# Four more products with tokens stationary, and activations turned by VectorE and small DMAs on the way

## Chip, cores and metric

One NeuronCore of a Trainium2 chip runs the whole program in one launch. The metric is the device time of one execution in microseconds (us).

## What is computed

A transformer block with sliding-window attention is followed by a second block on the same 256 tokens of width 2048. The second one is what the change touches:

```python
g = sigmoid(gate_logits + b_gate)                # gate_logits: 4096 of the columns of h @ w_in
merged = g[..., 0, :] * (y_mla @ w_mla_proj) + g[..., 1, :] * (y_diff @ w_diff_proj)
x = x + merged @ w_out                           # 2048 x 2048
h2 = rmsnorm(x, ffn_norm_g)
x = x + (silu(h2 @ w_ffn_gate) * (h2 @ w_ffn_up)) @ w_ffn_down
return rmsnorm(x, final_norm_g)
```

All data is float32. A product is made of three passes on TensorE: both operands are split into a high part and a rest ("hi", "lo"), and hi·hi, lo·hi and hi·lo are added up in PSUM.

## The kernel before

**Weights.** 5440 tiles of 128x128 come from HBM in the order in which the program asks for them, as 340 chunks of 16 tiles (1 MB, queue of SP). `Weights.cut` makes of each chunk two halves of 8 tiles: ACT writes `w_hi` (L84), DVE writes `w_lo` (L85). There are four buffers of each, so the cast of a half waits until PE is done with the half four before it. Nothing on TensorE runs without both.

**Two forms of product.** `gemm` and `gemm4` (L319, L329) hold the weights stationary. The activations move, transposed (features on partitions) with hi and lo of all 256 tokens side by side: `w_hi` goes against 512 columns, `w_lo` against the 256 of hi, which is two matmuls for a tile of weights. Results come out with features on partitions. `gemm_nat` with `nat3` (L367, L378) holds the activations of 128 tokens stationary, and 512 columns of weights move: six matmuls of 512 columns for four tiles (three passes, two blocks of tokens). Results come out with tokens on partitions. They must be turned before they can be stationary operands of the next product.

**Turning.** `moved` (L434) issues 16 DMAs of 32x128 on POOL's queue; with a DVE transpose inside 32x32 blocks ahead of it, this turns a 128x512 tile.

**Order around the change.** 512 tiles of gate, 256 of `mla`, 256 of `diff` and 256 of `out` use the first form, the `ffn` (1408 tiles) and `down` (704) the second. Gate strips of 128 features are evacuated by `total`, `scaled` and `gate` (L390, L395, L874); the loop at L880 interleaves the MLA and differential attention with these products through `between`, to which generators are added that emit a piece of work every few tiles. After `diff` a result is gated, added to the MLA part and split into `mg` (L919 to L932). After `out` (L938 to L946), each strip is added to the residual, scaled with the norm's gains and split into `h3_*`, the moving operand of the ffn stage; no turn is needed, since `h` is already there with features on partitions, and its 128-token slices serve as stationary operands. `after_out` (L950) sums the squares on PE, takes the root on POOL, and turns the residual (`x_t` to `x2n`) during the ffn. There, `split_act` (L967) splits the turned products (`act_hi`, `act_lo`).

The framework's scheduler fixes each engine's own order of instructions ahead of the run; the engine follows it strictly.

Of the kernel before, what the change touches and what calls it, by code (L numbers as in the profile page):

```python
# [14 lines left out]
P = 128  # L15
# [152 lines left out]


@with_exitstack  # L170
def block_kernel(ctx, tc, order, w, x01, xt, bc, fg, cst, out):
# [10 lines left out]
    def unit(name, dt=F32):  # L182
        return up.tile([P, 512], dt, name=name, tag="u", bufs=NU)
# [7 lines left out]
    def half(t, i):  # L191
        return t[:, (i % 2) * S:(i % 2) * S + S]
# [185 lines left out]
    def gemm_nat(name, col, acts):  # L378
# [492 lines left out]
    hb = const.tile([P, 32], F32, name="hb")  # L871
    nc.vector.tensor_scalar(out=hb, in0=colt[:, B_GATE:B_GATE + 32], scalar1=0.5, scalar2=None, op0=ALU.mult)

    def gate(m, o):  # L874
        ps = gemm("gate", m, h)
        scaled(o, ps, rb_2)
        nc.scalar.activation(out=o, in_=o, func=AF.Tanh, scale=0.5, bias=hb[:, m:m + 1])

    mer = []
    for u in range(4):  # L880
        qk = []
        for c in (0, 16):
            for i in range(4):
                ps = gemm("dqk", c + 4 * u + i, h)
                if i % 2 == 0:
                    qk.append(unit("qk_d"))
                scaled(half(qk[-1], i), ps, rb_2)
        pp = gemm_nat("dv", u * 512, h)
        v = []
        for tb in range(2):  # L890
            vh, vl = unit("v_hi", F32R), unit("v_lo", F32R)
            nc.scalar.activation(out=vh, in_=pp[tb], func=AF.Copy, scale=r_2[:, tb:tb + 1])
            nc.vector.scalar_tensor_tensor(out=vl, in0=pp[tb], scalar=r_2[:, tb:tb + 1], in1=vh.bitcast(F32),
                                           op0=ALU.mult, op1=ALU.subtract)
            v.append((vh, vl))
        if u == 0:
            between.drain()
            between.every, between.apart = 8, 3
        for i in range(2):
            between.add(attend_d(2 * u + i, qk[i], qk[2 + i], [(half(a, i), half(b, i)) for a, b in v]))  # L900
        if u == 0:
            for m in range(16):
                if m % 2 == 0:
                    t2, m2 = unit("gate"), unit("m")
                gate(m, half(t2, m))
                ps = gemm("mla", m, y_m)
                t = half(m2, m)
                total(t, ps)
                nc.vector.scalar_tensor_tensor(out=t, in0=half(t2, m), scalar=1.0, in1=t, op0=ALU.add, op1=ALU.mult)
                mer.append(t)  # L910

    gates = []
    for m in range(16):
        if m % 2 == 0:
            t2 = unit("gate")
        gate(16 + m, half(t2, m))
        gates.append(half(t2, m))
    between.drain()
    mg = []  # L919
    for m in range(16):  # L920
        ps = gemm("diff", m, y_d)
        if m % 2 == 0:
            t2 = unit("md")
        t = half(t2, m)
        total(t, ps)
        nc.vector.scalar_tensor_tensor(out=t, in0=gates[m], scalar=1.0, in1=t, op0=ALU.add, op1=ALU.mult)
        tt(t, t, mer[m], ALU.add)
        hl = unit(f"mg{m}", F32R)
        nc.scalar.activation(out=hl[:, 0:S], in_=t, func=AF.Copy, scale=0.5)
# [18 lines left out]
    x2n = []  # L948

    def after_out():  # L950
        yield
        nc.vector.tensor_copy(out=r_3, in_=rstd(sq.sums(), D))
        for cb in range(4):
            for tb in range(2):
                yield 8 if x2n else 3
                tr = unit("x2_t")
                for i in range(4):
                    nc.vector.transpose(
                        out=tr.rearrange("p (a m j) -> p a m j", a=4, m=4)[:, :, i, :],
                        in_=x2[4 * cb + i][:, tb * P:tb * P + P].rearrange("p (a j) -> p a j", a=4))  # L960
                x2n.append(moved(tr, "x2n"))

    between.every, between.apart = 16, 1
    between.add(after_out())
    act = [None] * KF

    def split_act(u, parts):  # L967
        yield 5
        hls = []
        for t in parts:  # L970
            t = t.rearrange("p (a g i) -> p g a i", a=4, g=4)
            hi, lo = unit("act_hi", F32R), unit("act_lo", F32R)
            nc.scalar.copy(out=hi.rearrange("p (g a i) -> p g a i", a=4, g=4), in_=t)
            tt(lo.rearrange("p (g a i) -> p g a i", a=4, g=4), t,
               hi.bitcast(F32).rearrange("p (g a i) -> p g a i", a=4, g=4), ALU.subtract)
            hls.append((hi, lo))
        for k in range(4):
            q = slice(k * P, k * P + P)
            act[4 * u + k] = [(hi[:, q], lo[:, q]) for hi, lo in hls]

    for u in range(KF // 4):

        parts = []
        for tb, ps in enumerate(gemm_nat("ffn", u * 512, h)):
# [3 lines left out]
        for tb, ps in enumerate(gemm_nat("ffn", DFF + u * 512, h)):  # L988
            z = parts[tb]
            tt(z, ps, z, ALU.mult)  # L990
            tr = unit("ffn_t")
            nc.vector.transpose(out=tr, in_=z)
            parts[tb] = moved(tr, "ffn_m")
        between.add(split_act(u, parts))
# [96 lines left out]
def _matrices(i):  # L1091

    pairs = []
    for j in range(16):
        kt = j // 8
        for hd in (16 * kt + j % 8, 16 * kt + 8 + j % 8):
            pairs.extend(range(hd * 64, hd * 64 + 64))
    pairs = np.array(pairs)
    in_a, in_2 = i["w_in_a"][0], i["w_in_2"][0]
    uq = i["w_uq_2"][0].reshape(768, 16, 192)  # L1100
    ukv = i["w_ukv_2"][0].reshape(512, 16, 256)
    kpe = in_2[:, 1280:1344]
    ffn = np.concatenate([i["w_ffn_gate_2"][0], i["w_ffn_up_2"][0]], axis=1)[:, _quarters(2 * DFF)]
    return {
        "in_a": np.concatenate([in_a[:, :2048][:, pairs], in_a[:, 2048:2560], in_a[:, 2560:][:, pairs]], axis=1),
        "out_a": i["w_out_a"][0][pairs],
        "in_2": in_2[:, :1280],
        "kpe": np.concatenate([kpe, kpe], axis=1),
        "dqk": in_2[:, 1344:5440],
        "dv": in_2[:, 5440:7488],  # L1110
        "gate": in_2[:, 7488:],
        "uq": np.concatenate([uq[:, :, :128].reshape(768, -1), uq[:, :, 128:].reshape(768, -1)], axis=1),
        "uk": ukv[:, :, :128].reshape(512, -1),
        "uv": ukv[:, :, 128:].reshape(512, -1),
        "mla": i["w_mla_proj_2"][0],
        "diff": i["w_diff_proj_2"][0],
        "out": i["w_out_2"][0],
        "ffn": ffn,
        "down": i["w_ffn_down_2"][0][:, _quarters(D)],
    }  # L1120
# [36 lines left out]
```

## Time and profile before

| | us |
|---|---|
| median of three runs (2012.25 to 2013.1) | 2012.4 |
| the profiled execution | 2012.29 |
| its span, first to last instruction | 2010.4 |
| PE busy in it | 1991.8 |
| DVE, ACT, POOL busy | 1265.3, 1036.5, 253.4 |

The span is the sum over a chain of work that ends with the last instruction. A stage can be read by itself: with the borders of the stages (the first matmul on the next operand), the profile gives for each the length, how long every engine was busy, and the number of instructions. Where PE is busy for the whole stage, the stage's length is that of its matmuls; a wait that PE gets there is added to the end of the program.

### The profile page before, as it was taken

To read this page: it belongs to the slowest core of one execution; us is meant where nothing else is said; L and a number is where in the kernel's file an instruction comes from. 1 tells how busy PE (TensorE), PEld (TensorE's weight loads), DVE (VectorE), ACT (ScalarE), POOL (GpSimd) and SP (SyncE) were. 2 spreads that over 40 slices of the span, in tenths; PEclk is the share of its full clock that TensorE was granted. 3 is DMA by queue.
4 is the path that set the end of the run, shared out by engine and by line. 5 is a ranking of instruction groups with operands and counts; after the bars stand their busy time and mean duration, and the time that the engine had idled before them with its cause. 6 is when DMAs were issued, how large, how long until landed. Compare 5 with 4: busy or idle time off the path is not lost.

```text
span 2010.4 us, 27424 instructions
## 1 busy us (share of the span) xinstructions
PE 1991.8 (99%) x10600; PEld 1703.7 (85%) x10600; DVE 1265.3 (63%) x2026; ACT 1036.5 (52%) x1681; POOL 253.4 (13%) x505
## 2 busy tenths in 40 slices
PE   9999999999999999999999999999999999999997
PEld 8888888888888888888888888888888888888886
DVE  7778766887857555566575767655555555554543
ACT  6777655656546444455465445544444444434443
POOL 0000000000000000000000000154555543330000
PEclk9999999999999999999999999999999999999999
DMA  7444455444344555545545555565566555565552
GB/s 301 153 145 148 168 207 180 161 153 147 131 174 163 191 189 190 194 163 181 181 160 191 187 195 189 184 222 204 207 217 216 208 206 208 209 220 190 196 200 85
DMA packets 68596, 372.68 MB, mean 185 GB/s; under 512 B 13745, under 2 KB 21937, under 8 KB 25329
## 3 DMA queue, kind: packets, MB, share of 16 engines
q1 hardware_dynamic: 51552, 359.76, 50.0%
q0 software_dynamic: 15760, 9.21, 1.6%
q10 hardware_dynamic: 1152, 1.97, 0.3%
q8 instruction: 83, 1.36, 0.3%
q14 instruction: 49, 0.39, 0.1%
HBM read 360.91 MB, written 2.10 MB: 181 GB/s over the span
## 4 chain that ended last, share of the span: by engine, by line
PE 96%; DVE 2%; ACT 1%; issue 1%; DMA 0%; POOL 0%; POOLq 0%; SPq 0%; ACTq 0%
PE ps_g L198 89%; PE ps_s L198 4%; PE ps_t L198 2%; PE ps_t L426 1%; DVE rope_t L201 1%; DVE w_lo L85 0%; DVE k_n L201 0%; DVE q_r L201 0%; DMA w_raw<-w 0%; ACT w_hi L84 0%; PE ps_t L865 0%; ACT prob L417 0%; PE ps_t L841 0%; DVE prob L411 0%; DVE y_m L235 0%
## 5 line engine op out<-in xcount | busy, mean ns | idle before, releaser
L85 DVE TENSOR_TENSOR w_lo<-w_raw,w_hi 128x1024 fp32r<-128x1024 f32 (+1 forms) x677 | 824.0, 1219 | 471.3 <-ACT w_hi L84 457.5
L84 ACT CAST w_hi<-w_raw 128x1024 fp32r<-128x1024 f32 (+1 forms) x677 | 708.7, 1048 | 571.5 <-PE ps_g L198 513.5
L198 PE MATMUL ps_g<-w_hi,h 128*128 128x512 f32 x1664 | 513.5, 389 | 0.0
L198 PE MATMUL ps_g<-h,w_hi 128*128 128x512 f32 x1672 | 410.3, 393 | 0.6 <-DVE h L238 0.6
L198 PEld LDWEIGHTS ps_g<-w_hi,h 128*128 128x128 f32 x1664 | 312.3, 188 | 64.9
L198 PEld LDWEIGHTS ps_g<-h,w_hi 128*128 128x128 f32 x1672 | 306.2, 188 | 63.1 <-issue 3.5
L198 PE MATMUL ps_g<-w_lo,h 128*128 128x512 f32 x832 | 323.7, 389 | 0.0
L198 PE MATMUL ps_g<-h,w_lo 128*128 128x256 f32 x1672 | 223.1, 284 | 0.0
L198 PEld LDWEIGHTS ps_g<-h,w_lo 128*128 128x128 f32 x1672 | 214.3, 191 | 10.4 <-issue 3.2
L439 POOL DMA_DIRECT2D ffn_m<-ffn_t x352 | 172.3, 497 | 222.8 <-ACT w_hi L84 86.1
L198 PEld LDWEIGHTS ps_g<-w_lo,h 128*128 128x128 f32 x832 | 156.2, 188 | 32.4
L279 POOL TENSOR_TENSOR rstd<-ms,mhalf 128x2 f32<-128x2 f32 x14 | 14.2, 1012 | 1217.2 <-DVE ms L274 1199.6
L198 PE MATMUL ps_g<-w_hi,act_hi 128*128 128x512 f32 x344 | 133.8, 389 | 0.0
L198 PE MATMUL ps_g<-w_lo,act_hi 128*128 128x512 f32 x344 | 133.8, 389 | 0.0
L198 PE MATMUL ps_g<-w_hi,act_lo 128*128 128x512 f32 x344 | 133.8, 389 | 0.0
L198 PEld LDWEIGHTS ps_g<-w_lo,act_hi 128*128 128x128 f32 x344 | 64.6, 188 | 13.5
L198 PEld LDWEIGHTS ps_g<-w_hi,act_hi 128*128 128x128 f32 x344 | 64.6, 188 | 13.5
L198 PEld LDWEIGHTS ps_g<-w_hi,act_lo 128*128 128x128 f32 x344 | 64.6, 188 | 13.2
L439 POOL DMA_DIRECT2D x2n<-x_t x128 | 62.7, 497 | 31.7 <-ACT ffn L986 15.6
L198 PE MATMUL ps_g<-y_m,w_hi 128*128 128x512 f32 x256 | 63.8, 391 | 0.0
L198 PE MATMUL ps_g<-y_d,w_hi 128*128 128x512 f32 x256 | 61.2, 391 | 0.0
L198 PE MATMUL ps_g<-g,w_hi 128*128 128x512 f32 (+1 forms) x240 | 57.8, 377 | 0.0
(254 smaller groups left out, 2011.6 us busy)
## 6 DMA issues: line engine op xcount, KB each, us to landing
w_raw<-w SPq DMA_DIRECT2D x337, 1024.0 KB, 4.8
ffn_m<-ffn_t POOLq DMA_DIRECT2D x352, 16.0 KB, 4.1
w_raw<-w SPq DMA_DIRECT2D x5, 512.0 KB, 7.6
x2n<-x_t POOLq DMA_DIRECT2D x128, 16.0 KB, 4.1
x_t<-xt SPq DMA_DIRECT2D x7, 256.0 KB, 7.6
fgt<-fg POOLq DMA_DIRECT2D x4, 256.0 KB, 3.9
out<-x2n SPq DMA_DIRECT2D x4, 256.0 KB, 3.1
out<-x2n ACTq DMA_DIRECT2D x4, 256.0 KB, 3.5
```

What stands on the lines that cost most here:

```text
L84: a = nc.scalar.copy(out=hi[:, q], in_=src[:, q])
L85: b = nc.vector.tensor_tensor(out=lo[:, q], in0=src[:, q], in1=hi.bitcast(F32)[:, q], op=ALU.subtract)
L198: nc.tensor.matmul(out=o, lhsT=a, rhs=b, start=start, stop=stop, skip_group_check=True)
L201: nc.vector.tensor_tensor(out=o, in0=a, in1=b, op=op)
L279: nc.gpsimd.tensor_tensor(out=r, in0=t, in1=mhalf[:, 0:n], op=ALU.pow)
L426: nc.tensor.transpose(out=ps[:, j * P:j * P + P], in_=p[:, j * P:j * P + P], identity=ident)
L439: nc.gpsimd.dma_start(out=o[32 * b:32 * b + 32, a * P:a * P + P], in_=tr[32 * a:32 * a + 32, b * P:b * P + P])
```

## The change

- Gate, `mla`, `diff` and `out` use `gemm_nat`; weights of these four are reordered so that the features of a strip of 512 come out in the order that the later turn wants.
- The gate's bias is no column any more but a row, copied to all partitions. `row` fetches 128x512 (256 KB) on POOL's queue into a buffer; the norm's gains ahead of the ffn (`R_FFN`) come in the same way.
- `turn_residual` turns the residual `x1` to `x1n` during the gate and `mla` products (DVE transposes and 16 DMAs, eight times). Before, the same work on `x2` was in the ffn.
- A strip of `diff` is gated and added with tokens on partitions, then `turned` (one transpose and 16 DMAs for a block of tokens, 32 a strip) and split by `split_turned` into `t_hi` and `t_lo`, the stationary operands of `out`. A strip of `out` goes the same way (`residual_2`), with the gains multiplied in (`x2g`), to become those of the ffn. It takes four strips of turned activations to make all 16 pieces along k.
- The first product after such a turn (`out`, and the gate and up product of the ffn) begins with two strips side by side: `gemm_nats` runs pieces 0 to 11 along k of both, then pieces 12 to 15 of both. 
- The sums of squares are collected by ACT (`accum_out`), and four matmuls that added them up are gone.

```diff
+    def gemm_nats(name, cols, acts, late):
+        banks = [[bank("g") for _ in range(2)] for _ in cols]
+        n = len(acts)
...
+        for ks in (range(late), range(late, n)):
+            for col, pp in zip(cols, banks):
+                for k in ks:
+                    hi, lo = W.take(name, k * P, col, 4)
+                    for tb in range(2):
+                        nat3(pp[tb], acts[k], tb, hi, lo, k == 0, k == n - 1)
+                    between.tiles(4)
+        return banks
+    def turned(z):
+        tr = unit("turn")
+        nc.vector.transpose(out=tr, in_=z)
+        return moved(tr, "turned")
+    def split_turned(acts, k0, parts):
+        yield 5
...
+            nc.scalar.copy(out=oh, in_=t)
+            tt(ol, t, oh.bitcast(F32), ALU.subtract)
...
+    def row(base, i):
+        t = unit("row")
+        nc.gpsimd.dma_start(out=t, in_=rw[:, base + i * 512:base + i * 512 + 512])
+        return t
...
-    mg = []
-    for m in range(16):
-        ps = gemm("diff", m, y_d)
...
+    for i in range(4):
+        parts = []
+        for tb, ps in enumerate(gemm_nat("diff", i * 512, y_d)):
+            t = gates[i][tb]
+            gated(t, ps)
+            tt(t, t, mer[i][tb], ALU.add)
+            parts.append(turned(t))
+        between.add(split_turned(mg, 4 * i, parts))
...
-    for m, ps in blocks("out", 0, 16, mg):
-        t = x1[m]
-        tt(t, t, ps[:, 0:S], ALU.add)
-        tt(t, t, ps[:, S:], ALU.add)
-        x2.append(t)
-        hl = unit(f"h3_{m}", F32R)
-        split_scaled(t, gcol(G_FFN, m), hl)
-        h.append(hl)
-        sq.add(t)
+    def residual_2(cb, pp):
+        g = row(R_FFN, cb)
+        parts = []
+        for tb, ps in enumerate(pp):
+            t = x2n[2 * cb + tb]
+            nc.vector.scalar_tensor_tensor(out=t, in0=ps, scalar=0.5, in1=t, op0=ALU.mult, op1=ALU.add)
+            z = unit("x2g")
+            nc.scalar.activation(out=z, in_=t, func=AF.Square, accum_out=sums3[:, 4 * tb + cb:4 * tb + cb + 1])
+            z = unit("x2g")
+            tt(z, t, g, ALU.mult)
+            parts.append(turned(z))
+        between.add(split_turned(h, 4 * cb, parts))
+
+    for cb, pp in enumerate(gemm_nats("out", [0, 512], mg, 12)):
+        residual_2(cb, pp)
+    for cb in (2, 3):
+        residual_2(cb, gemm_nat("out", cb * 512, mg))
...
+        if u == 0:
+            pg, pu = gemm_nats("ffn", [0, DFF], h, 12)
```

What the order of the instructions says of the place where `out` ends and the ffn begins. First POOL, whose queue carries the small DMAs. Before, from the last attention norms on to the first DMAs of the ffn:

```order
L279 TENSOR_TENSOR rstd_10067<-ms_10065,mhalf_115 128x2
L279 TENSOR_TENSOR rstd_12374<-ms_12372,mhalf_115 128x2
L439 DMA x2n_12490<-x2_t_12485 32x128 x16
L439 DMA ffn_m_12612<-ffn_t_12610 32x128 x16
L439 DMA ffn_m_12632<-ffn_t_12630 32x128 x16
```

Of the change, from the first strip of `out` to the last:

```order
L482 DMA row_11342<-rw 128x512
L454 DMA turned_11351<-turn_11349 32x128 x16
L454 DMA turned_11375<-turn_11373 32x128 x16
L482 DMA row_11392<-rw 128x512
L454 DMA turned_11401<-turn_11399 32x128 x16
L454 DMA turned_11425<-turn_11423 32x128 x16
L482 DMA row_11580<-rw 128x512
L454 DMA turned_11589<-turn_11587 32x128 x16
L454 DMA turned_11613<-turn_11611 32x128 x16
L482 DMA row_11784<-rw 128x512
L454 DMA turned_11793<-turn_11791 32x128 x16
L454 DMA turned_11817<-turn_11815 32x128 x16
```

The four strips of `out` each have a fetch of gains and 32 moves here, and each fetch stands behind the moves of the strip before it. None of these was there before.

Then DVE, before, around the first half of weights of the ffn (`w_lo_12338`, with the last strips of `out` still to be evacuated):

```order
L85 TENSOR_TENSOR w_lo_12338<-w_raw_12335,w_hi_12337 128x1024
L201 TENSOR_TENSOR y_2858<-y_2858,ps_g_12247 128x256 x2
L85 TENSOR_TENSOR w_lo_12354<-w_raw_12335,w_hi_12353 128x1024
L238 SCALAR_TENSOR_TENSOR h3_15_12292<-y_2858,x01t_75,h3_15_12292 128x256
L201 TENSOR_TENSOR sq_11660<-sq_11660,sq_12295 128x256
```

DVE of the change, from the first half of weights of the ffn (half 416 of the program, counted from 0; the three `w_lo` after it are 417, 418 and 419); `row_11580` is the gains of the third strip of `out`, `ps_g_11630` and `ps_g_11631` are the fourth strip, and `t_lo_11701` is the first strip's rest, an operand of the first product of the ffn:

```order
L86 TENSOR_TENSOR w_lo_11850<-w_raw_11847,w_hi_11849 128x1024
L202 TENSOR_TENSOR x2g_11585<-x1n_7340,row_11580 128x512
L461 STREAM_TRANSPOSE turn_11587<-x2g_11585 128x512
L86 TENSOR_TENSOR w_lo_11866<-w_raw_11847,w_hi_11865 128x1024
L202 TENSOR_TENSOR x2g_11609<-x1n_7504,row_11580 128x512
L461 STREAM_TRANSPOSE turn_11611<-x2g_11609 128x512
L86 TENSOR_TENSOR w_lo_11884<-w_raw_11881,w_hi_11883 128x1024
L994 SCALAR_TENSOR_TENSOR x1n_7670<-ps_g_11630,x1n_7670 128x512
L994 SCALAR_TENSOR_TENSOR x1n_7844<-ps_g_11631,x1n_7844 128x512
L86 TENSOR_TENSOR w_lo_11900<-w_raw_11881,w_hi_11899 128x1024
L202 TENSOR_TENSOR t_lo_11701<-turned_11351,t_hi_11700 128x512
L202 TENSOR_TENSOR t_lo_11705<-turned_11375,t_hi_11704 128x512
```

Between weights and operands of the next stage now stand instructions of the third and fourth strip of `out`. The first matmuls of the ffn on PE are, of the change:

```order
L199 MATMUL ps_g_11843<-w_hi_11849,t_hi_11700 128x512
L199 MATMUL ps_g_11843<-w_lo_11850,t_hi_11700 128x512
L199 MATMUL ps_g_11843<-w_hi_11849,t_lo_11701 128x512
L199 MATMUL ps_g_11844<-w_hi_11849,t_hi_11704 128x512
L199 MATMUL ps_g_11844<-w_lo_11850,t_hi_11704 128x512
```

Its third matmul takes the rest of the first turned strip, where before all operands were slices of `h3_*`.

## Rows read from the trace of the kernel before

**Rows 1.** The page's head and its busy times of the engines: busy us (share of the span) and number of instructions.
```profile
span 2010.4 us, 27424 instructions
PE 1991.8 (99%) x10600; PEld 1703.7 (85%) x10600; DVE 1265.3 (63%) x2026; ACT 1036.5 (52%) x1681; POOL 253.4 (13%) x505
```
**Rows 2.** The chain that ended last, by engine.
```profile
PE 96%; DVE 2%; ACT 1%; issue 1%; DMA 0%; POOL 0%; POOLq 0%; SPq 0%; ACTq 0%
```
**Rows 3.** Stages: start and end, length, then busy us (instructions) of PE, PEld, DVE, ACT and POOL, the granted clock, the DMA share and GB/s. In order: attention with the gate and `mla` products, the 256 tiles of `diff`, the 256 of `out`, the 1408 of the ffn.
```profile
516.00:1100.42 584.42, 584.04 (x3307) 511.90 (x3307) 367.95 (x588) 305.56 (x517) 9.14 (x8) 1.00 0.50 178
1100.42:1189.49 89.07, 89.07 (x514) 78.72 (x512) 62.08 (x94) 43.19 (x64) 0.00 (x0) 1.00 0.53 189
1189.49:1278.56 89.07, 89.07 (x513) 78.67 (x512) 62.11 (x95) 44.99 (x64) 0.00 (x0) 1.00 0.53 191
1278.56:1757.86 479.30, 479.30 (x2118) 396.88 (x2117) 259.24 (x275) 211.79 (x221) 220.04 (x449) 1.00 0.60 209
```
**Rows 4.** PE in order of time, at the end of `diff` and at the border of `out` and ffn: start, length of the group (to the end of its last matmul), what, and how many.
```profile
1185.74 2.08 PE L198 MATMUL ps_g<-y_d,w_lo 128*128 128x256 f32 x16
1187.65 2.00 PE L198 MATMUL ps_g<-y_d,w_hi 128*128 128x512 f32 x8
...
1276.80 2.00 PE L198 MATMUL ps_g<-mg,w_hi 128*128 128x512 f32 x8
1278.64 0.39 PE L198 MATMUL ps_g<-w_hi,h 128*128 128x512 f32 x1
```
**Rows 5.** Groups of instructions from 1100 to 1760 us: line, engine, operation, tile and shapes, count, busy us, mean ns of one, idle time before them and what ended it.
```profile
L85 DVE TENSOR_TENSOR w_lo<-w_raw,w_hi 128x1024 fp32r<-128x1024 f32 x241 | 294.5, 1222 | 231.7 <-ACT w_hi L84 231.5
L84 ACT CAST w_hi<-w_raw 128x1024 fp32r<-128x1024 f32 x241 | 253.7, 1053 | 301.5 <-PE ps_g L198 286.8 <-PE ps_s L198 12.8 <-ACT sq L254 1.3
L439 POOL DMA_DIRECT2D x2n<-x_t x128 | 62.7, 497 | 31.7 <-ACT ffn L986 15.6 <-DMA x2n<-x_t 9.2 <-issue 2.8
L992 DVE STREAM_TRANSPOSE ffn_t<-ffn 128x512 f32<-128x512 f32 x21 | 14.7, 701 | 0.0
L201 DVE TENSOR_TENSOR act_lo<-ffn_m,act_hi 128x512 fp32r<-128x512 f32 x20 | 13.7, 684 | 0.0
L973 ACT CAST act_hi<-ffn_m 128x512 fp32r<-128x512 f32 x20 | 12.4, 618 | 0.1
L958 DVE STREAM_TRANSPOSE x_t<-y 128x128 f32<-128x128 f32 x32 | 7.1, 277 | 0.0
L198 PE MATMUL ps_t<-ones,sq 128*128 128x1 f32 x4 | 0.5, 228 | 0.0
```
**Rows 6.** The same view of DVE, 1760 us to the end: evacuations of `down` with tokens on partitions, and a product with a row of gains.
```profile
L1005 DVE SCALAR_TENSOR_TENSOR x2n<-ps_g,r,x2n 128x512 f32<-128x512 f32 x7 | 5.0, 745 | 3.1 <-PE ps_g L198 3.1
L201 DVE TENSOR_TENSOR x2n<-x2n,fgt 128x512 f32<-128x512 f32 x6 | 3.9, 684 | 0.0
```
**Rows 7.** POOL in order of time, two turns of a strip in the ffn, each of 32 moves: start, length of the group, number of issues, and in brackets the idle time before the group and what ended it.
```profile
1368.33 4.40 POOL L439 DMA_DIRECT2D ffn_m<-ffn_t  x9 [13.57 <-ACT w_hi L84]
1373.64 0.50 POOL L439 DMA_DIRECT2D ffn_m<-ffn_t  x1 [0.90 <-DMA ffn_m<-ffn_t]
1374.82 3.92 POOL L439 DMA_DIRECT2D ffn_m<-ffn_t  x8 [0.69 <-DMA ffn_m<-ffn_t]
1379.48 3.91 POOL L439 DMA_DIRECT2D ffn_m<-ffn_t  x8 [0.75 <-DMA ffn_m<-ffn_t]
1383.91 0.50 POOL L439 DMA_DIRECT2D ffn_m<-ffn_t  x1 [0.51 <-DMA ffn_m<-ffn_t]
1385.15 2.44 POOL L439 DMA_DIRECT2D ffn_m<-ffn_t  x5 [0.74 <-DMA ffn_m<-ffn_t]
...
1498.64 4.89 POOL L439 DMA_DIRECT2D ffn_m<-ffn_t  x10 [13.46 <-DVE ffn_t L992]
...
1515.62 2.94 POOL L439 DMA_DIRECT2D ffn_m<-ffn_t  x6 [1.40 <-DMA ffn_m<-ffn_t]
```
**Rows 8.** The views of the tiles `ffn_m` (moves of 16 KB) and `fgt` (256 KB, the final norm's gains): issues with ns of one (min/median/max), and the time from issue to landing.
```profile
L439 POOL DMA_DIRECT2D ffn_m<-ffn_t x352: 496/496/501, 1324.9 to 1780.1; - x176
DMA to landing us min/median/max: 1.6/4.1/6.7
...
L1000 POOL DMA_DIRECT2D fgt<-fg x4: 536/540/566, 1780.5 to 1783.6; - x4
DMA to landing us min/median/max: 3.1/3.9/4.0
```
**Rows 9.** PE at the start of the program, in order of time as in rows 4.
```profile
1.07 5.35 PE L219 MATMUL ps_warm<-ones 128*128 128x128 f32 x26 [1.07 <-DVE ones L205]
6.17 0.71 PE L198 MATMUL ps_g<-h,w_hi 128*128 128x512 f32 x2
```
**Rows 10.** The end of the program in steps of 2 us, columns as in rows 3; the clock stands behind POOL.
```profile
1998.00:2000.00 2.00, 0.00 (x0) 0.00 (x0) 0.75 (x3) 0.89 (x3) 0.55 (x1) 1.00 0.38 138
2000.00:2002.00 2.00, 0.00 (x0) 0.00 (x0) 0.77 (x2) 0.95 (x2) 0.00 (x0) 1.00 0.55 193
2002.00:2004.00 2.00, 0.00 (x0) 0.00 (x0) 0.00 (x0) 0.00 (x0) 0.00 (x0) 0.62 0.99 315
```

More of the change, by code (lines that the diff above doesn't have):

```diff
@@ L170, in block_kernel @@
 @with_exitstack
-def block_kernel(ctx, tc, order, w, x01, xt, bc, fg, cst, out):
+def block_kernel(ctx, tc, order, w, x01, xt, bc, rw, cst, out):
     nc = tc.nc
@@ L441, in moved @@
         return o
+    def turned(z):
[4 more added lines that the diff above has]
+        yield 5
+        hls = []
+        for t in parts:
+            t = t.rearrange("p (a g i) -> p g a i", a=4, g=4)
+            hi, lo = unit("t_hi", F32R), unit("t_lo", F32R)
+            oh, ol = (o.rearrange("p (g a i) -> p g a i", a=4, g=4) for o in (hi, lo))
+            nc.scalar.copy(out=oh, in_=t)
+            tt(ol, t, oh.bitcast(F32), ALU.subtract)
+            hls.append((hi, lo))
+        for g in range(4):
+            q = slice(g * P, g * P + P)
+            acts[k0 + g] = [(hi[:, q], lo[:, q]) for hi, lo in hls]
+    def row(base, i):
+        t = unit("row")
+        nc.gpsimd.dma_start(out=t, in_=rw[:, base + i * 512:base + i * 512 + 512])
+        return t
     sq = Squares(8)
@@ L869, in attend_d, with gate, gated, turn_residual @@
             split_scaled(half(ps, dt), g_d[:, dt:dt + 1], y_d[2 * head + dt])
[L871 to L877, printed above, removed]
+    def gate(i):
+        b = row(R_GATE, i)
+        o = []
+        for tb, ps in enumerate(gemm_nat("gate", i * 512, h)):
+            t = unit("gate")
+            nc.vector.scalar_tensor_tensor(out=t, in0=ps, scalar=r_2[:, tb:tb + 1], in1=b, op0=ALU.mult, op1=ALU.add)
+            nc.scalar.activation(out=t, in_=t, func=AF.Tanh, scale=0.5)
+            o.append(t)
+        return o
+    def gated(t, ps):
+        nc.vector.scalar_tensor_tensor(out=t, in0=t, scalar=1.0, in1=ps, op0=ALU.add, op1=ALU.mult)
+    x1n = []
+    def turn_residual():
+        for cb in range(4):
+            for tb in range(2):
+                yield 8
+                tr = unit("turn")
+                for i in range(4):
+                    nc.vector.transpose(
+                        out=tr.rearrange("p (a m j) -> p a m j", a=4, m=4)[:, :, i, :],
+                        in_=x1[4 * cb + i][:, tb * P:tb * P + P].rearrange("p (a j) -> p a j", a=4))
+                x1n.append(moved(tr, "x1n"))
     mer = []
@@ L901, in block_kernel @@
         if u == 0:
-            for m in range(16):
[L903 to L917, printed above, removed]
@@ L963, in block_kernel @@
-    between.every, between.apart = 16, 1
-    between.add(after_out())
-    act = [None] * KF
[L967 to L979, printed above, removed]
+            between.add(turn_residual())
@@ new lines, in block_kernel @@
+            for i in range(4):
+                mer.append(gate(i))
+                for t, ps in zip(mer[i], gemm_nat("mla", i * 512, y_m)):
+                    gated(t, ps)
+    gates = [gate(4 + i) for i in range(4)]
+    between.drain()
+    between.every, between.apart = 16, 1
+    mg = [None] * KD
+    for i in range(4):
+        parts = []
+        for tb, ps in enumerate(gemm_nat("diff", i * 512, y_d)):
+            t = gates[i][tb]
+            gated(t, ps)
+            tt(t, t, mer[i][tb], ALU.add)
+            parts.append(turned(t))
+        between.add(split_turned(mg, 4 * i, parts))
@@ new lines, in block_kernel @@
+    sums3 = sm("sums3", 8)
+    x2n = x1n
+    h = [None] * KD
+    def residual_2(cb, pp):
[10 more added lines that the diff above has]
+        between.add(split_turned(h, 4 * cb, parts))
@@ new lines, in block_kernel @@
+    for cb, pp in enumerate(gemm_nats("out", [0, 512], mg, 12)):
+        residual_2(cb, pp)
+    for cb in (2, 3):
+        residual_2(cb, gemm_nat("out", cb * 512, mg))
+    r_3 = const.tile([P, 2], F32, name="r_3")
+    ms = sm("ms", 2)
+    for tb in range(2):
+        nc.vector.tensor_reduce(out=ms[:, tb:tb + 1], in_=sums3[:, 4 * tb:4 * tb + 4], op=ALU.add,
+                                axis=mybir.AxisListType.X)
+    nc.vector.tensor_copy(out=r_3, in_=rstd(ms, D))
+    act = [None] * KF
@@ L981, in block_kernel @@
     for u in range(KF // 4):
+        if u == 0:
+            pg, pu = gemm_nats("ffn", [0, DFF], h, 12)
+        else:
+            pg = gemm_nat("ffn", u * 512, h)
         parts = []
-        for tb, ps in enumerate(gemm_nat("ffn", u * 512, h)):
+        for tb, ps in enumerate(pg):
             z = unit("ffn")
@@ L987, in block_kernel @@
             parts.append(z)
[L988 to L994, printed above, removed]
+        if u:
+            pu = gemm_nat("ffn", DFF + u * 512, h)
+        for tb, ps in enumerate(pu):
+            tt(parts[tb], ps, parts[tb], ALU.mult)
+            parts[tb] = turned(parts[tb])
+        between.add(split_turned(act, 4 * u, parts))
     tot = sm("tot", 10)
@@ L998, in block_kernel @@
     for cb in range(4):
-        t = unit("fgt")
-        nc.gpsimd.dma_start(out=t, in_=fg[:, cb * 512:cb * 512 + 512])
-        fgt.append(t)
+        fgt.append(row(R_FINAL, cb))
     def residual(cb, tb, ps, cols=slice(0, 512), i=0):
@@ L1114, in _matrices @@
         "uv": ukv[:, :, 128:].reshape(512, -1),
-        "mla": i["w_mla_proj_2"][0],
-        "diff": i["w_diff_proj_2"][0],
-        "out": i["w_out_2"][0],
+        "mla": i["w_mla_proj_2"][0][:, _quarters(D)],
+        "diff": i["w_diff_proj_2"][0][:, _quarters(D)],
+        "out": i["w_out_2"][0][:, _quarters(D)],
         "ffn": ffn,
@@ L1144 @@
     with tile.TileContext(nc) as tc:
-        block_kernel(tc, order, ap["w"], ap["x01"], ap["xt"], ap["bc"], ap["fg"], ap["cst"], out)
+        block_kernel(tc, order, ap["w"], ap["x01"], ap["xt"], ap["bc"], ap["rw"], ap["cst"], out)
     assert len(order) <= N_CHUNK * CH, len(order)
```

40 lines of the change are left out of this document (7 added, 33 removed).

## The prediction

> **What bounds the kernel.** I read the page's head first: PE is busy for 1991.8 of 2010.4 us, and no other engine is near it [rows 1]. The chain that ended last says the same; 96% of it is PE [rows 2]. So two things can move the time: fewer or cheaper matmuls, and new waits of PE. The stages show where there is room. From the attention on, PE is busy for the whole of every stage at a clock of 1.00, while DVE works 62 of 89 us and POOL nothing in `diff` and `out` [rows 3]. Every wait the change makes there is added to the end; work on DVE, ACT and POOL is free only as long as it delivers in time. The sum is made against the profiled execution: 2012.3 us, a span of 2010.4 and 1.9 around it. The median of three runs, 2012.4, is the same for this purpose. What a measurement can tell from no change is 0.2%, 4 us.
>
> **Cheaper matmuls: -10.1 us.** `diff` and `out` take 89.07 us for 256 tiles in the old form, 0.3479 us a tile; the ffn takes 479.30 for 1408 in the new, 0.3404 [rows 3]. The 0.0075 us between them, times the 1280 tiles of gate, `mla`, `diff` and `out`, is 9.7 us (for gate and `mla` I assume the price of `diff`, which has the same two matmuls a tile). The cause is visible in order of time: eight matmuls of 512 columns take 2.00 us to the end of the last, seven spacings and its 0.39, so 0.23 a spacing; sixteen of 256 take 2.08, fifteen spacings and 0.28, so 0.12 [rows 4]. Against 0.213 and 0.107 for the columns alone at 2.4 GHz, each matmul costs some 13 to 16 ns more, whatever its width, and a tile goes from 2 matmuls to 1.5. Four matmuls for the sum of squares go too: 0.4 us at the most for matmul and its changes of weights [rows 5].
>
> A rule speaks against this gain. The Trainium skill, page "TensorE: Matmul & The Clock Gate", section "Back-to-back issue gap", gives an isolated gap of N/2.4 + 2.5 ns; by it a tile would go from 325.0 to 323.8 ns and the 1280 tiles would give 1.6 us, 8 less than the rows do. The trace differs, with 227 ns a matmul of 512 in the ffn stage (0.3404/1.5), so I take the rows.
>
> **Work that moves and stays covered: 0 to 1 us.** The turn of the residual goes from the ffn (32 transposes of 277 ns and 128 moves of 497, [rows 5]) to the stage of gate and `mla`, where DVE is idle for over 200 of 584 us and POOL for nearly all [rows 3]; only the attention's own POOL work (eight pieces of 1.1 us) can queue behind a group of moves. The gate rows (eight fetches on POOL's queue) stand there too. Evacuations with tokens on partitions cost DVE 745 ns for 128x512 [rows 6] in place of several of 128x256; DVE keeps room. At the joint of `diff` and `out`, the last strip of `diff` needs about 4.3 us on DVE, 32 moves at 19.3 (below) and a split, in all some 26.6 us, while PE has pieces 0 to 11 of two strips, 12 halves of weights at 2.72 us (8 tiles at 0.3404), 32.7 us. The next half of weights queues on ACT and DVE behind that split and is ready at 29.6 us against 29.9 wanted. Covered, with nothing to spare.
>
> **The joint of `out` and ffn: +23 us.** Here cover fails, by the order of POOL and DVE. The terms, from rows:
> - a move takes POOL 0.497 us, but 32 take 19.3 (1368.33 to 1387.59; another strip 1498.64 to 1518.56, 19.9): after eight or nine in a row POOL waits for an earlier move to land [rows 7]. They land 4.1 us after issue in the median, 1.6 to 6.7 [rows 8].
> - a fetch of gains (256 KB): POOL 0.5, landing 3.9 by `fgt` [rows 8]; 4.4 in all.
> - DVE: `x1n` 0.75 and `x2g` 0.68 [rows 6], transpose 0.70, `t_lo` 0.68, `w_lo` 1.22; ACT: `t_hi` 0.62, `w_hi` 1.05 [rows 5].
>
> Count from the end of half 397, when strip 0 of `out` is complete. PE has 18 halves of `out` left, 49.0 us. DVE evacuates and turns strip 0 (twice 0.75 + 0.68 + 0.70, 4.3 us), its 32 moves end at 23.6, and only then can POOL fetch the gains of strip 1: 28.0. Then `x2g`, a `w_lo` and the transpose, 30.6; 32 moves, 49.9; gains of strip 2, 54.3. DVE's order has `x2g` of strip 2 ahead of `w_lo` of halves 417 to 419 and of `t_lo_11701`, without which the ffn has two matmuls to run: two `x2g`, two transposes, three `w_lo`, two `x1n` and `t_lo`, 8.6 us, so 62.9. PE finished `out` at 49.0 and its two matmuls take 0.45: **a first stall of 13.4 us**. In it `w_hi` of 419 and the first `t_hi` on ACT are ready at 50.7; DVE ends last.
>
> PE now has halves 416 to 419, 10.7 us to 73.6, and next wants half 422. Strip 2 is turned by 55.7; its moves end at 75.0, the gains of strip 3 land at 79.4, and `x2g`, a transpose and `w_lo` of 422 follow, 82.0: **a second stall of 8.4 us**. After it I find only 0.9 us of waits (a late `w_lo`, the `t_lo` of the last strips), since pieces 12 to 15 come as late as half 428.
>
> The clock: behind the last matmuls the granted clock is 1.00 in two slices of 2 us and 0.62 in the third, on its way from 2.4 to 1.2 GHz [rows 10], so I expect it at the lower level after 13.4 us of idle time, and after 8.4. What a resumption costs, the trace bounds: below by nothing, above by 2.6 us, half of the 5.1 us between the first matmul of the program and one at full spacing [rows 9]. After the first stall it shortens the second wait, so it counts once; I take 1.5.
>
> Sum: -9.7 - 0.4 + 13.4 + 8.4 + 0.9 + 1.5 = **+14 us, 2026**.
>
> Bounds of the joint. With moves that never wait (15.9 for 32) each round is 3.4 us shorter; `t_lo` is ready at 56.1, the stalls are 6.6 and 5.0, with the small ones 12.5, and the time 2015 (2017 with the clock). With 19.9 a strip and fetches that take the longest landing of a move, 6.7, each of three rounds is 3.4 longer: stalls of 20.2 and 11.8, and with a clock lost twice 2040.
>
> **Rivals.**
> 1. *Landings near their shortest* (the side of no change or faster). In the ffn the queue is full of weights; were moves and fetches to land as soon as the shortest of them do, 1.6 and 3.1 us [rows 8], POOL would never wait, a fetch costs 3.6, the stalls are 5.0 and 4.2, and the time is 2012; with fetches at 1.6 too, the first stall sinks to 2.6 (`t_hi` and `t_lo` still stand behind the casts of half 419, which wait for PE), the second to 2.7, and the time is 2008.4. It decides below 2 us of landing. For it: DMA is lighter here (share 0.53 in `out` against 0.60 in the ffn, [rows 3]). Against it: medians of 4.1 and 3.9. The Trainium skill, page "DMA: Bandwidth & Descriptors", section on the anatomy of a gpsimd DMA, fits 2.0 us + bytes/436e3; by it a move would land after 2.0 and a fetch after 2.6, and the time would be an estimated 2011. The trace's medians stand against it. Chance 0.12, of that 0.04 faster.
> 2. *Moves at full rate, fetches as `fgt`*: the low bound, 2015 to 2017. For it: eight or nine in a row go without a wait. Against: every strip shown takes 19 us or more. Chance 0.13, about half of it within 4 us of before.
> 3. *The joint is covered*: something in the order lets PE go on, only the form counts, 2002. The only support is that POOL and DVE are idle on average; the order is strict. Chance 0.04.
> 4. *More is late*: the joint at `diff` loses its 0.3 us of slack (each microsecond longer in the moves is one of stall), or the form gives next to nothing because the moving weights cost more than in the ffn (8 us less gain, 2034), or the joint comes out at its upper bound (2040): 2034 and more. Chance 0.09.
> 5. *The change doesn't do what it says* would mean a row where strips side by side give no cover; at `diff` to `out` they do, so this is part of 4.
>
> **The numbers.** The forecast, both stalls with 2018 to 2034, has 0.62, and the likeliest time is 2026. Faster by over 0.2% (below 2008.4): 0.04 of rival 1 and all of rival 3, with 0.01 for what I don't see, 0.09. Within 0.2%: 0.08 of rival 1 and half of rival 2, 0.14. Slower: the rest, 0.77. The range 2012 to 2036 leaves out about 0.12 below and 0.07 above.
>
> **What would show it.** Right: tiles of gate, `mla`, `diff` and `out` at 0.340 us outside of waits; `diff` as a stage near 87.2 us; PE idle near the start of the ffn for 13 us until `t_lo`, and some 11 us later for 8 until `w_lo`, with the chain there through POOL's moves, `row` and `x2g`; 32 moves in 19 us; a clock at the lower level after the stalls. Wrong: a new-form tile at 0.348 takes away the gain; moves that land after 2 us, or a DVE that is not held by `x2g` at the end of `out`, take away the stalls; idle time of PE ahead of `out` would mean that I missed a wait.

## The result

The changed kernel takes 2020.18 us, median of six runs (2018.31 to 2021.8), against 2012.33 before; the ratio is 1.0037, 95% interval 1.0024 to 1.005. It is slower, by 7.9 us; 13.7 were forecast, and the range held it. The profiled execution is the longest of the six (2021.8); its own rows are used below, and they stand 9.5 us above those of before.

The head of the page [rows 1], and the chain by engine [rows 2], which now reaches back only to the place of the last wait, since the chain is followed through what released it:

```profile
span 2019.9 us, 26449 instructions
PE 1989.4 (98%) x9956; PEld 1673.7 (83%) x9956; DVE 1230.5 (61%) x1892; ACT 1009.0 (50%) x1585; POOL 383.4 (19%) x773
...
PE 35%; issue 0%; DMA 0%; DVE 0%; ACT 0%; POOLq 0%; POOL 0%; DVEq 0%
```

The stages, with the columns of [rows 3]; the borders are again the first matmul on the next operand (the last one counts the matmuls of 1408 tiles and ends where `down` begins):

```profile
516.00:1095.68 579.68, 579.30 (x2926) 492.13 (x2925) 349.55 (x551) 285.22 (x453) 74.44 (x144) 1.00 0.53 187
1095.68:1182.72 87.04, 87.04 (x385) 72.07 (x384) 53.15 (x57) 36.88 (x38) 46.45 (x95) 1.00 0.62 211
1182.72:1269.77 87.05, 87.05 (x385) 71.88 (x383) 50.01 (x54) 39.46 (x48) 47.14 (x98) 1.00 0.61 212
1269.77:1771.62 501.85, 485.22 (x2114) 399.61 (x2114) 264.65 (x261) 216.49 (x231) 191.16 (x390) 0.98 0.58 200
```

`diff` and `out` are 87.04 and 87.05 us where they were 89.07: 0.340 us a tile. The stage with gate and `mla` gains 5.6 (from the first matmul on `c` in the second block, 408.4 before and 409.2 now, to the border). The ffn is 22.6 us longer, and 16.6 of it PE is idle. The waits of PE from 500 us on, those over 0.4 us (engine and line, what it waited for, us in total, times, longest):

```profile
PE ps_g L199 <- DVE t_lo L202: 9.9, 1, 9.9
PE ps_g L199 <- DVE w_lo L86: 5.1, 1, 5.1
PE ps_g L199 <- ACT t_hi L472: 1.7, 1, 1.7
```

Each stands where the walk put it. PE in order of time, from the end of `out` to behind the second wait (start, length; in brackets the idle time and its end):

```profile
1269.54 0.39 PE L199 MATMUL ps_g<-w_hi,t_lo 128*128 128x512 f32 x1
1271.58 0.50 PE L199 MATMUL ps_g<-w_hi,t_hi 128*128 128x512 f32 x1 [1.65 <-ACT t_hi L472]
1271.92 0.40 PE L199 MATMUL ps_g<-w_lo,t_hi 128*128 128x512 f32 x1
1282.18 0.79 PE L199 MATMUL ps_g<-w_hi,t_lo 128*128 128x512 f32 x1 [9.87 <-DVE t_lo L202]
1282.78 0.63 PE L199 MATMUL ps_g<-w_hi,t_hi 128*128 128x512 f32 x1
1283.20 0.63 PE L199 MATMUL ps_g<-w_lo,t_hi 128*128 128x512 f32 x1
...
1288.59 0.40 PE L199 MATMUL ps_g<-w_hi,t_lo 128*128 128x512 f32 x1
...
1301.14 0.80 PE L199 MATMUL ps_g<-w_lo,t_hi 128*128 128x512 f32 x1 [5.10 <-DVE w_lo L86]
...
1305.52 0.39 PE L199 MATMUL ps_g<-w_hi,t_lo 128*128 128x512 f32 x1
```

Two matmuls run, then PE waits for `t_lo`; behind each wait the spacing is 0.43 us instead of 0.23 for a while (1282.78 to 1283.20 and on). POOL and DVE in the same stretch say where the waits come from:

```profile
1251.56 3.92 POOL L454 DMA_DIRECT2D turned<-turn  x8 [5.46 <-PE ps_g L199]
...
1267.80 3.44 POOL L454 DMA_DIRECT2D turned<-turn  x7 [0.20 <-issue]
1271.22 0.57 POOL L482 DMA_DIRECT2D row<-rw  x1
1276.19 4.41 POOL L454 DMA_DIRECT2D turned<-turn  x9 [4.39 <-issue]
...
1293.88 0.57 POOL L482 DMA_DIRECT2D row<-rw  x1
```

```profile
1274.20 0.69 DVE L202 TENSOR_TENSOR x2g<-x1n,row 128x512 f32<-128x512 f32 x1 [10.08 <-DMA row<-rw]
...
1281.45 2.49 DVE L202 TENSOR_TENSOR t_lo<-turned,t_hi 128x512 fp32r<-128x512 f32 x4
...
1298.54 0.69 DVE L202 TENSOR_TENSOR x2g<-x1n,row 128x512 f32<-128x512 f32 x1 [5.76 <-DMA row<-rw]
```

The fetch for strip 2 leaves POOL at 1271.22, when the 32 moves of strip 1 are done (19.7 us from their first, as the strips in [rows 7]). DVE has stood still for 10.08 us at `x2g`, and `t_lo`, whose strip's last move was issued at 1243, comes 7.3 us behind it.

### The profile page after: what moved, and what is told of

The parts are those of the page before. It is cut to its first block, busy times and chain, and to the rows that moved or that the text cites. A ratio compares the mean times of both kernels' runs of the same rounds, so it can differ in the third digit from the quotient of the medians.

```text
span 2019.9 us, 26449 instructions
## 1 busy us (share of the span) xinstructions
PE 1989.4 (98%) x9956; PEld 1673.7 (83%) x9956; DVE 1230.5 (61%) x1892; ACT 1009.0 (50%) x1585; POOL 383.4 (19%) x773
## 5 line engine op out<-in xcount | busy, mean ns | idle before, releaser
L199 PE MATMUL ps_g<-w_hi,t_lo 128*128 128x512 f32 x1176 | 459.6, 391 | 9.9 <-DVE t_lo L202 9.9
L199 PE MATMUL ps_g<-w_lo,t_hi 128*128 128x512 f32 x1176 | 459.5, 391 | 5.1 <-DVE w_lo L86 5.1
L199 PE MATMUL ps_g<-w_hi,t_hi 128*128 128x512 f32 x1176 | 459.7, 391 | 1.7 <-ACT t_hi L472 1.7
L454 POOL DMA_DIRECT2D turned<-turn x608 | 297.4, 497 | 459.1 <-DVE turn L461 135.8
L199 PEld LDWEIGHTS ps_g<-w_hi,t_lo 128*128 128x128 f32 x1176 | 222.0, 189 | 57.3 <-DVE t_lo L202 11.3
L199 PEld LDWEIGHTS ps_g<-w_lo,t_hi 128*128 128x128 f32 x1176 | 222.0, 189 | 51.8 <-DVE w_lo L86 5.5
L199 PEld LDWEIGHTS ps_g<-w_hi,t_hi 128*128 128x128 f32 x1176 | 221.9, 189 | 48.5 <-ACT t_hi L472 2.4
L199 PE MATMUL ps_g<-w_hi,h 128*128 128x512 f32 x768 | 241.4, 391 | 0.0
L199 PEld LDWEIGHTS ps_g<-w_hi,h 128*128 128x128 f32 x768 | 144.2, 188 | 29.9
L199 PE MATMUL ps_g<-w_lo,h 128*128 128x512 f32 x384 | 149.5, 389 | 0.0
```

Source lines behind the costliest of these rows:

```text
L199: nc.tensor.matmul(out=o, lhsT=a, rhs=b, start=start, stop=stop, skip_group_check=True)
```

## Where the end of the program differs

PE's last matmul ends 13.8 us later than before (2011.45 and 1997.69), but the span is only 9.5 longer: the tail behind PE shrank from 12.7 to 8.5 us. The last long `DRAIN` instruction of POOL's sequencer, which begins with POOL's last operation and which the closing semaphores of all engines wait for, lasts 10.64 us before (to 2009.64, while SP is done with the output at 2005.46) and 2.88 in the changed kernel, where SP ends last. The forecast has nothing of this.

## Experiments

The changed kernel is the base where nothing else is said. Times are medians; "before" was timed beside each set (2012.3 to 2012.9).

**e1: fetches early.**

```diff
     gates = [gate(4 + i) for i in range(4)]
+    gains = [row(R_FFN, cb) for cb in range(4)]
...
-        g = row(R_FFN, cb)
+        g = gains[cb]
```

> All four fetches of the ffn gains are issued on POOL's queue ahead of the diff products instead of one behind the moves of each strip; nothing else differs. Theory 1 (the fetch behind the moves, with x2g of strip 2 ahead of t_lo on DVE, makes the waits): the 11.5 and 5.1 us waits of PE shrink to 2 to 6 us in all, the slow clock after them mostly goes; 14 to 19 us less than the changed kernel, 2001 to 2007. Theory 2 (the rate of the moves alone makes them): the strips are still turned one after the other at 18 to 19 us each, waits of 12 us or more stay, 2013 or more.

Measured: 2011.86 us (ratio 0.9999, 0.999 to 1.0007), no difference from before, and 8.3 less than the changed kernel. Its waits of PE, and the DMA issues from 1220 to 1290 us (KB each, median us to landing):

```profile
PE ps_g L199 <- ACT t_hi L472: 5.9, 1, 5.9
PE ps_g L199 <- DVE w_lo L86: 3.7, 4, 1.8
PE ps_g L199 <- ACT w_hi L85: 1.2, 1, 1.2
```

```profile
w_raw<-w SPq DMA_DIRECT2D x12, 1024.0 KB, 5.1
turned<-turn POOLq DMA_DIRECT2D x101, 16.0 KB, 3.9
```

The long wait for `t_lo` is gone, although DVE still has both `x2g` of the third strip ahead of it: it was the late fetch, through this order, that made the wait. But 10.8 us of shorter waits stay: the strips are now turned without a pause, at 19 to 21 us each, and the third comes 5.9 us late. Both theories missed: mine promised 2001 to 2007, and the rate of the moves alone 2013.

**e2: half of the moves on ACT's queue**, fetches late.

```diff
-                nc.gpsimd.dma_start(out=o[32 * b:32 * b + 32, a * P:a * P + P],
+                (other if other and b % 2 else nc.gpsimd).dma_start(out=o[32 * b:32 * b + 32, a * P:a * P + P],
...
-            parts.append(turned(z))
+            parts.append(turned(z, nc.scalar))
```

> Fetches stay where the change has them; half of the moves behind out go through ACT's queue. Theory 1: the chain fetch, x2g, moves is shortened by the moves' half, some 8 us in each of three rounds, so the waits go as well, 2002 to 2008, unless ACT's own casts come late behind issues that wait for a transpose. Theory 2: the same or better, 2000 to 2004. If ACT is held: waits of PE for w_hi of 2 us or more each strip, 2008 to 2014.

Measured: 2018.95 us (1.0029, 1.0018 to 1.0039), above every expectation; 1.2 us of it is a longer tail (POOL's drain is 7.54 us here). The waits, the DMA issues from 1220 to 1290 us, and ACT in order of time:

```profile
PE ps_g L199 <- ACT w_hi L85: 6.5, 2, 4.4
PE ps_g L199 <- ACT t_hi L472: 5.5, 1, 5.5
PE ps_g L199 <- DVE w_lo L86: 1.9, 4, 0.8
```

```profile
w_raw<-w SPq DMA_DIRECT2D x10, 1024.0 KB, 5.2
turned<-turn POOLq DMA_DIRECT2D x56, 16.0 KB, 4.3
turned<-turn ACTq DMA_DIRECT2D x55, 16.0 KB, 4.5
...
```

```profile
1265.56 6.81 ACTq L454 DMA_DIRECT2D turned<-turn  x7
...
1273.22 1.04 ACT L85 CAST w_hi<-w_raw 128x1024 fp32r<-128x1024 f32 x1
```

`t_lo` no longer bounds PE, but ACT, which is in order too, is held at its issues (6.81 us for these seven), and the weights' casts behind them come late. The moves land no sooner.

**e3: early fetches, and the third strip wanted later** (in the first product of the ffn, pieces 0 to 7 of both strips, then 8 to 11, then 12 to 15).

```diff
-    def gemm_nats(name, cols, acts, late):
-        for ks in (range(late), range(late, n)):
+        for k0, k1 in zip((0,) + late, late + (n,)):
+            ks = range(k0, k1)
...
-            pg, pu = gemm_nats("ffn", [0, DFF], h, 12)
+            pg, pu = gemm_nats("ffn", [0, DFF], h, (8, 12))
```

> Fetches early, and the first two strips of the ffn run pieces 0 to 7 of both, then 8 to 11 of both, then 12 to 15, so that the third strip is wanted 11 us later. Theory 1: what is left of the waits after e1 are those for strips 2 and 3; with this they sink to 0 to 4 us, 1998 to 2006, and the time is no longer than that of e1. Theory 2: a few us less than e1, over 2008.

Measured: 2012.22 us (0.9998, 0.9989 to 1.0006), no better than e1. The wait moved:

```profile
PE ps_g L199 <- ACT w_hi L85: 6.5, 2, 6.0
PE ps_g L199 <- DVE w_lo L86: 3.0, 5, 0.8
```

```profile
1300.80 0.62 ACT L473 CAST t_hi<-turned 128x512 fp32r<-128x512 f32 x1 [8.46 <-DMA turned<-turn]
1301.33 1.99 ACT L85 CAST w_hi<-w_raw 128x1024 fp32r<-128x1024 f32 x2
```

PE now gets past the third strip, but ACT's order has the first `t_hi` of the fourth (1300.80, after 8.46 us of standing still for its moves) ahead of the casts of weights that PE wants earlier. A miss for my expectation, and the same lesson as the kernel's own.

**e5: early fetches, and half of the moves of `diff` and `out` on SP's queue.**

```diff
-            parts.append(turned(t))
+            parts.append(turned(t, nc.sync))
...
-            parts.append(turned(z))
+            parts.append(turned(z, nc.sync))
```

(with the edits of e1, and `moved` as in e2)

> Fetches early as in e1, and half of the moves of the diff and out strips issued on SP's queue, which carries the weights four chunks ahead. If what was left in e1 (10 us of waits) is the rate of the moves, PE is released: waits of 0 to 3 us, PE's last matmul at 1988 to 1992 us, time 1998 to 2006 with a tail of 8 to 12 us. If the moves were only a symptom (ACT or DVE being late by their own work), 7 us or more of waits stay and PE ends at 1996 or later. If SP is held by a wait for a transpose, PE waits for w_hi.

Measured: **2000.52 us** (0.9941, 0.9929 to 0.9954), the fastest of all kernels here: 12 us less than before, 19.7 less than the changed kernel. Waits, and the DMA issues from 1215 to 1290 us:

```profile
PE ps_g L199 <- DVE w_lo L86: 1.5, 2, 0.8
PE ps_g L199 <- ACT w_hi L85: 0.4, 1, 0.4
```

```profile
w_raw<-w SPq DMA_DIRECT2D x13, 1024.0 KB, 6.9
turned<-turn SPq DMA_DIRECT2D x64, 16.0 KB, 2.0
turned<-turn POOLq DMA_DIRECT2D x64, 16.0 KB, 1.8
```

The moves land in half the time, on both queues: SP issues them between the loads of weights, so that beside most of them none is in flight (the first of `out`, right behind two loads, need 4.9 us, falling to 2.2 at the thirteenth on SP's queue). And each queue has only 16 moves of a strip, which SP issues in 10.6 us (1252.69 to 1263.3), where POOL's 32 took 19.7.

**e9: the same with the fetches late**, where the change has them.

> Fetches stay where the change has them, one behind the moves of each strip; half of the moves of the diff and out strips go through SP's queue as in e5. With e1 and e5 and the changed kernel this makes a square of two factors. If the waits come from a chain of moves and fetches together, halving the moves' share brings each round from 23 to some 15 us, all four strips are turned in time, and the waits are 0 to 4 us: 2000 to 2004. If a late fetch is a cause by itself (x2g holds DVE, and SP is held behind a transpose): 6 us or more of waits stay, 2006 or more. e2, the same with ACT's queue, was at 2019; were that due to the fetches and not to ACT, this would be as slow.

Measured: 2001.2 us (0.994, 0.9926 to 0.9954).

```profile
PE ps_g L199 <- DVE w_lo L86: 1.5, 2, 0.8
...
PE ps_g L199 <- ACT w_hi L85: 0.3, 1, 0.3
```

With e1 and e5 the square is complete: late fetches cost 8.3 us where the moves go through one queue and 0.7 where they go through two; the one queue costs 11.3 us with early fetches and 19.0 with late ones. In all four DVE has the `x2g` of the third strip ahead of the first `t_lo` of the ffn. The fetch behind the moves hurts only by lengthening a chain that the moves had made too long already.

**e11: all those moves on SP's queue.** The edit of e9 with `(other or nc.gpsimd).dma_start(...)`.

> As e9, but all moves of the diff and out strips go on SP's queue and none on POOL's, so that no queue is relieved by sharing; only the place changes: the moves stand between the loads of weights instead of beside them. In e5 a move landed after 2.0 us, in e1 after 3.9, and in e2 (half on ACT's queue) after 4.4. If what counts is that no load of weights is in flight beside the moves: landing near 2 us again, 32 moves in some 16 to 18 us, waits of 0 to 8 us in all, 2000 to 2008. If what counts is that two queues share 32 moves: landing as in the changed kernel, 32 moves in 19 to 22 us, waits of 8 us or more, 2009 or more; weights held up by a queue that is busy with moves would add to it and show as PE waiting for w_hi.

Measured: 2080.68 us (1.0339, 1.0325 to 1.0353). The waits, and the DMA issues from 1200 to 1360 us:

```profile
PE ps_g L199 <- ACT w_hi L85: 69.0, 5, 39.5
```

```profile
w_raw<-w SPq DMA_DIRECT2D x21, 1024.0 KB, 5.9
turned<-turn SPq DMA_DIRECT2D x143, 16.0 KB, 1.8
...
```

The landing is that of the first expectation, the time is not; the hold-up that the second one named, PE waiting for `w_hi`, is 69.0 us: at 0.63 us from issue to issue, a queue full of moves starves the weights. But the question of landing has its answer: with one queue and nothing beside them, 32 moves in a row land after 1.8 us each. The first of those right behind two loads of weights need 7.7, 7.3, 7.0, and so on down to 2.1 at the eighth (issued 1141.46 to 1148.80). So it is the megabytes ahead of it that a move waits for. For the length of a strip it matters little here. Its 32 moves, from the first issue to the end of the last, take 18 to 22 us from one queue with slow landings (the changed kernel and e1), 20 to 23 from one with quick ones (e11), 11 to 14 from two with slow ones (e2, `out`) and 10 to 11 from two with quick ones (e5). So the second queue is what halves a strip; what quick landings would save on POOL's queue alone, at 0.5 us an issue, no run shows.

**e10: the first strips one after the other.** What the rest of the change, the strips side by side, is worth.

```diff
                 for k in ks:
+                    while acts[k] is None:
+                        between.tick()
...
-    for cb, pp in enumerate(gemm_nats("out", [0, 512], mg, 12)):
+    for cb, pp in enumerate(gemm_nats("out", [0, 512], mg, 16)):
...
-            pg, pu = gemm_nats("ffn", [0, DFF], h, 12)
+            pg, pu = gemm_nats("ffn", [0, DFF], h, 16)
```

> The changed kernel with the first strips of out and ffn one after the other instead of side by side (pieces 0 to 15 of the first strip, then the second); a split is emitted at the latest where its piece is wanted. By the walk of the prediction: at diff to out the pieces 12 to 15 are wanted after 6 halves, 16.3 us, and are ready after 26 to 27, a wait of about 10; at out to ffn the last strip is turned some 36 us after PE's end of out, of which 16 are covered, about 20; with two resumptions at the lower clock, less what the changed kernel waits now (17 and 4.5), 2026 to 2038. If side by side is worth nothing because the queue decides either way: 2018 to 2022.

Measured: 2029.57 us (1.0082, 1.0068 to 1.0097 against before), within the expectation: 9.4 us slower than the change. The waits are spread over both joints:

```profile
PE ps_g L199 <- ACT t_hi L474: 12.3, 5, 5.2
PE ps_g L199 <- DVE w_lo L86: 5.5, 2, 5.0
PE ps_g L199 <- DVE t_lo L202: 3.4, 1, 3.4
```

**e4, e6, e7, e8: the tail.** The kernel before, with 128, 32, 64 and 96 of the residual's moves in the ffn issued twice (n is 8, 2, 4, 6):

```diff
                 x2n.append(moved(tr, "x2n"))
+                if len(x2n) <= n:
+                    moved(tr, "x2n")
```

> The kernel before with the moves of the residual issued twice (128 more DMAs on POOL's queue in the ffn). It asks two things. Are such moves free where nothing waits for them: then PE is busy as before and the time is within 2 us of 2012.3. And what sets the 10.6 us of POOL's last drain instruction (2.9 in the changed kernel, which has 268 more DMAs): if it is the number of DMAs, the drain differs from 10.6 here; if it is what the rest of the program is, it stays at 10 to 11.

> The kernel before with 32 of the residual's moves issued twice (516 DMAs on POOL's queue; before 484, e4 612). Drains so far: 10.65 us at 484, 1.33 at 612, 7.54 at 688 (e2), 2.88 at 752. If the drain is a saw tooth of the number of DMAs, one that fits these four (period about 121, 0.082 us a DMA) gives 3.4 us here and a time near 2008.5; another that fits (period 96, 0.146) gives 1.3. If the drain doesn't follow the number of DMAs: 10 to 11, and 2012.3.

> As e6 with 64 moves issued twice (548 DMAs): the saw tooth gives 6.0 us by either period, which is the length at which the output's landing takes over, so about 2008.5. If not by number: 10 to 11, and 2012.3.

> As e6 with 96 moves issued twice (580 DMAs): the saw tooth of period 121 gives 8.6 us and about 2010.5; that of period 96 10.6 us and 2012.3. If not by number: 10 to 11, and 2012.3.

Measured, with the other kernels, by the number of DMAs on POOL's queue; the drain is that of the profiled execution, the time in a row of several kernels that of the first named (e5, the changed kernel), the last column a saw tooth of 0.0816 us a DMA and a period of 121 DMAs, set to e6, e8 and before:

```
kernel        DMAs on POOL   drain us   time us   saw tooth
before            484          10.64     2012.3     10.64
e11               496           1.74     2080.7      1.75
e6                516           3.38     2008.4      3.38
e7                548           5.99     2008.3      5.99
e8                580           8.60     2010.3      8.60
e4                612           1.33     2008.3      1.34
e5, e9            624           2.31     2000.5      2.32
e2                688           7.54     2019.0      7.54
changed, e1,
e3, e10           752           2.88     2020.2      2.89
```

More work on POOL makes the kernel before faster: 0.998 of its time with 128 more moves (0.9971 to 0.9988), 0.998 with 32 (0.997 to 0.9989). The moves themselves are free (PE's last matmul at 1997.89 in e4, 1997.69 before); the drain is shorter. It follows the number of DMAs alone in these thirteen kernels, unlike as they are. It costs what it exceeds some 6 us by, the time from POOL's last operation to the landing of the output: 4.2 us before, nothing with 548. What POOL does in it the runs don't show.

## Why the prediction was right, and where it was off

- **The form.** Forecast -9.7 us; measured -5.6 for gate and `mla`, -2.0 for `diff` and -2.0 for `out`, -9.6 in all. By the gap of an isolated matmul in the Trainium skill ("TensorE: Matmul & The Clock Gate", "Back-to-back issue gap") the gain would have been an estimated 1.6; the trace differs, with 87.04 us for 256 tiles, 227 ns a matmul of 512.
- **Covered work.** Right: PE is busy for the whole of `diff` and `out`, and at their joint nothing waits. There was nothing to spare, as said: e1 and e3, with as slow moves, wait 1.2 and 1.4 us there.
- **The first wait.** Forecast 13.4 from the end of `out` until `t_lo`, measured 11.5 (1.65 and 9.87). Counted from the end of half 397 (1220.8), strip 0 is turned at 22.9 (23.6 forecast), strip 1 at 50.4 (49.9), the gains of strip 2 land at 53.4 (54.3) and `t_lo` is there at 61.3 (62.9). The chain is the forecast one; the fetch took 3.0 instead of 4.4, and DVE ran its ten instructions in 7.9 us, not 8.6.
- **The second wait and the clock.** Forecast 8.4 and 1.5; measured 5.1 of waiting behind 2.6 of slow matmuls (13 at 0.43 us instead of 0.23), and 1.8 (nine of them) after it. The granted clock shows it: 0.50 in the last 6 us of the first wait and the 6 after it, 0.97 in the next 7 (columns as in [rows 3]).

```profile
1276.00:1282.00 6.00, 0.00 (x0) 0.00 (x0) 5.97 (x8) 0.00 (x0) 4.91 (x10) 0.50 0.58 199
1282.00:1288.00 6.00, 5.82 (x14) 4.56 (x15) 2.00 (x5) 1.04 (x1) 4.86 (x10) 0.50 0.58 199
1288.00:1295.00 7.00, 7.00 (x32) 5.73 (x31) 2.45 (x3) 3.35 (x6) 6.45 (x14) 0.97 0.26 55
```

  The slow stretch after the first wait only took from the second, as the text said. The joint was forecast at 24.2 us with the clock; the ffn stage is 22.6 longer: 16.6 of waits where 22.7 were forecast, 4.4 of slow matmuls, of which 2.6 came out of the second wait, and single wider spacings (the first behind the first wait is 0.60 us, 1282.18 to 1282.78).
- **The sum.** PE's last matmul was to come 14 us later, and comes 13.8 later in the profiled execution: 22.6 in the ffn less 9.6 by the form, and 0.8 from ahead of the stages that the change touches (the first matmul on `c` at 409.2 instead of 408.4, behind a few matmuls spaced 0.43 us near 344 us, where before has 0.23). The forecast has nothing of the 0.8, so that the fit to 0.2 us is partly luck. The forecast of the time was 5.8 us too high. 4.2 of it is what the forecast did not have: the tail of before is 4.2 us too long by POOL's drain, and the change, by its number of DMAs, happens to shorten it. The other 1.6 is the distance of the profiled execution from the median of its runs; the 0.8 may be part of it, and what the rest is was not shown. With equal tails (e7's 2008.3) the change is 11.9 us slower.
- **The rivals.** Quick landings (the first one) did not come in this kernel: 3.9 us for a move in the median, 3.5 for a row (4.1 and 3.9 in [rows 8]). DMA was no lighter in `out` either, with a share of 0.61 against 0.58 in the ffn. Of the 736 moves of 16 KB on POOL's queue, 22 have no load of weights in flight between issue and landing; they land after 1.6 us, the other 714 after 4.0 in the median. By the Trainium skill, "DMA: Bandwidth & Descriptors", on the anatomy of a gpsimd DMA, a move would take an estimated 2.0 us and a row 2.6; for the moves the trace comes near it only where no load is in flight. That rival's condition was named too vaguely, as a lighter load; it is the weights beside the moves. The third rival (the joint covered), priced at 2002, is where e9 comes out with a second queue, at 2001.2; in the change itself nothing covers the joint.

## What to carry to other kernels

A transfer that another instruction needs soon must not queue behind a batch on the same queue, and an instruction that waits must not stand on an in-order engine ahead of what the bounding engine wants next: price the chain in the order of each engine's own list, where idle shares say nothing. A batch of small moves is as long as the issues of its queue: a second queue halved it here, on an engine that the bounding engine does not wait for; on ACT's queue it held up the casts, and all of the batch on the queue of the loads starved them. Small moves also land late beside large loads (4 us instead of 1.6 to 1.8). And compare the tail behind the last matmul, before a gain or loss is put down to the change.

## What was not expected of the hardware

Between 484 and 752 DMAs, the last long drain of POOL grows by 0.0816 us with each DMA issued on its queue and falls back by 9.9 us three times, as a period of 121 DMAs has it; it was 1.33 to 10.64 us in these kernels. Of two saw teeth that fitted four values, the one of this period forecast 3.4, 6.0 and 8.6 for the next three, which came out at 3.38, 5.99 and 8.60. A move of 16 KB lands after 1.8 us by itself and after up to 7.7 directly behind two loads of 1 MB. A matmul of 512 columns is spaced 0.43 us at the lower clock and 0.23 at the higher.
